# Gate and up products of both feed-forwards by token, their result turned on TensorE, and the input's squares on ScalarE

## Chip, cores and metric

The kernel runs on one core of a Trainium2 chip. The metric is the device time of one execution in microseconds, the median of several runs. Shares and durations come from one profiled execution.

## What is computed

One layer of a streaming encoder on 256 tokens of width 2048, all in float32. The part that the change touches is the two feed-forwards, at the start and at the end:

```python
def rms_norm(x, g):
    y = x * lax.rsqrt(jnp.mean(x * x, axis=-1, keepdims=True) + RMS_EPS)
    return y * g

def swiglu_ffn(h, w_in, w_out):
    gate, up = jnp.split(h @ w_in, 2, axis=-1)      # w_in (2048, 2 * 5632)
    return (jax.nn.silu(gate) * up) @ w_out         # w_out (5632, 2048)

x = x + 0.5 * swiglu_ffn(rms_norm(x, ffn1_norm), ffn1_w_in, ffn1_w_out)
x = x + token_mixing(x)            # convolution and gated MLP, w_mix_in, w_mix_out
x = x + cross_attention(x, mem)    # four heads, w_q, w_k, w_v, w_o
x = x + 0.5 * swiglu_ffn(rms_norm(x, ffn2_norm), ffn2_w_in, ffn2_w_out)
out = rms_norm(x, final_norm)
```

## The kernel before

Every large product runs in float32r. Both operands are split into a high part and a low part that add up to the float32 value, and a product is the sum of three: high by high, high by low, low by high. `weights` (line 97) loads a weight tile of up to 128 x 1024 numbers (512 KB) on SyncE's queue into one of four `raw` buffers. ScalarE casts it to the high part (line 104), and VectorE subtracts for the low part (line 105), both into one of three `hl` buffers. The activations stand in SBUF by feature, `x_hl[:, k]` being 128 features by both parts by 256 tokens; the norm's gain is in them, and its inverse root is multiplied in after the product.

A product comes in three forms. `product` (line 115), which `gemm_t` uses, has 128 weight columns stationary. One matmul moves the 512 columns of both parts of x past the high weights, a second the 256 columns of the high part past the low weights; the result stands by feature, in two halves that are still to be added. `product_joint` (line 120) does the same as three matmuls of 256. `gemm_n` (line 150) has 128 tokens of x stationary and moves 512 weight columns, three matmuls for each k and half of the tokens; its result stands by token. `ffn2_w_out`, `w_mix_v` and `w_v` use it.

`swiglu_in` (line 245) makes a feed-forward's first stage. For each of 44 tiles of 128 hidden features it runs two `gemm_t`, gate and up, of 16 k each (two weight tiles each). The results are joined, multiplied by the inverse root, put through Silu, multiplied and split into `hA` and `hB`, the operands of the second product, all by feature and in operations of 256 columns on ScalarE and VectorE (lines 261 to 269). `first_pair` (line 279) does the first two products of feed-forward 1 while x arrives; GpSimd squares x there (lines 307 and 309), and a product by `ones` (line 208) sums the squares over partitions for the inverse root. Feed-forward 2 takes its sum of squares from `residual` (line 235) of the stage before.

PSUM has six buffers for accumulators (`ps`) and two for small things (`pa`). Small pieces of other work, such as the memory's squares in feed-forward 1 and the transposition of x in blocks of 32 in feed-forward 2 (line 709), are given out by `beside` after weight tiles. The order on each engine is made by a scheduler when the program is built. It follows the program's order, and may put an instruction earlier where an engine would be free.

Of the kernel before, what the change touches and what calls it, by code (L numbers as in the profile page):

```python
# [11 lines left out]
F32 = mybir.dt.float32  # L12
# [23 lines left out]
# columns of the packed per-channel parameters  # L36
# [25 lines left out]
def layer(ctx: ExitStack, tc: tile.TileContext, a: dict):  # L62
# [34 lines left out]
    def weights(src, kk, n, hl=None):  # L97
        """src [P, kk, n] in DRAM: both parts, each [P, kk, n]."""
# [16 lines left out]
    def product(acc, w_hi, w_lo, x_hl, first, last):  # L115
        """acc[:, 0] + acc[:, 1] += w.T @ x, x as [K, 2, n] of both parts."""
# [3 lines left out]
    def product_joint(acc, w_hi, w_lo, x_hl, first, last):  # L120
        """acc[:, 0] += w.T @ x"""
# [5 lines left out]
    def product_part(acc, w, k0, kk, x_hl, per, first, last, joint=False):  # L127
        """The part of a product by feature that k0 .. k0 + kk bring."""
# [6 lines left out]
    def gemm_t(w, x_hl, per=0.0, acc=None, ks=None, joint=False):  # L135
        """w [P, K, 128] in DRAM; x_hl(k) -> [P, 2, 256]: 128 outputs by 256 tokens."""
        return ahead([w], x_hl, per, [acc], ks, joint)[0]

    def ahead(ws, x_hl, per=0.0, accs=None, ks=None, joint=False, end=True):
        """Products of which each part of K is done for all before the next."""  # L140
# [4 lines left out]
        for i, (k0, kk) in enumerate(ks):  # L145
            for w, acc in zip(ws, accs):
                product_part(acc, w, k0, kk, x_hl, per, i == 0 and not started, end and i == len(ks) - 1, joint)
        return accs

    def gemm_n(w, x_hl, per=0.0):  # L150
        """w [P, K, 512] in DRAM: two tiles of 128 tokens by 512 outputs."""
        acc = [ps.tile([P, 2, 256], F32, name="acc").rearrange("p a b -> p (a b)") for _ in range(2)]
        nk = w.shape[1]
        for k0 in range(0, nk, 2):
            kk = min(2, nk - k0)
            hi, lo = weights(w[:, k0:k0 + kk, :], kk, 512)
            for k in range(kk):
                x = x_hl(k0 + k)
                for t in range(2):
# [3 lines left out]
                    nc.tensor.matmul(acc[t], lhsT=x[:, 1, s], rhs=hi[:, k], start=False, stop=k0 + k == nk - 1)  # L163
            beside(per)
        return acc

    def joined(acc, dst):
        """dst = acc[:, 0] + acc[:, 1]"""
# [16 lines left out]
    def inverse_root(dst, src, scale, eps):  # L185
        """dst = (src * scale + eps) ** -0.5, the table's root refined by a Newton step"""
# [18 lines left out]
    def over_partitions(acc):  # L205
        """The sum of acc over partitions, on each partition, in PSUM."""
# [17 lines left out]
    def gained(dst, k, x, g):  # L224
        """dst[:, k] = both parts of x * g"""
# [19 lines left out]
    def swiglu_in(x_hl, root, w_in, hA, hB, first, hold, per):  # L245
        """root() gives the norm's inverse root, after the products of `hold` pairs more than the first."""
        waiting = []
        r = None
        for j in range(KF):
            if j == 0:  # L250
                accs = first()
            else:
                accs = [gemm_t(w_in[j, i], lambda k: x_hl[:, k], per=per if j > 4 else 0.0) for i in range(2)]
            waiting.append((j, accs))
            if j < hold:
                continue
            if r is None:
                r = root()
            for i, (gate, up) in waiting:
                tg = ev.tile([P, T], F32, name="tg")  # L260
                tu = ev.tile([P, T], F32, name="tu")
                joined(gate, tg)
                nc.vector.tensor_tensor(out=tg, in0=tg, in1=r, op=ALU.mult)
                nc.scalar.activation(out=tg, in_=tg, func=AF.Silu)
                joined(up, tu)
                nc.vector.tensor_tensor(out=tu, in0=tu, in1=r, op=ALU.mult)
                nc.vector.tensor_tensor(out=tu, in0=tu, in1=tg, op=ALU.mult)
                dst = hA[:, i] if i < KD else hB[:, i - KD]
                split(dst[:, 0], dst[:, 1], tu)
            waiting = []  # L270
# [8 lines left out]
    def first_pair():  # L279
        """The first two products, as x arrives."""  # L280
        accs = [ps.tile([P, 2, 256], F32, name="acc") for _ in range(2)]
        head = PV["mix_norm"][0]
        for k0 in range(0, KD, 2):
            nc.sync.dma_start(out=xT[:, k0:k0 + 2], in_=a["xT"][:, k0:k0 + 2])
            if k0 == 0:
                nc.sync.dma_start(out=pv[:, :head], in_=a["pv"][:, :head])
            if k0 == 4:
                nc.sync.dma_start(out=pv[:, head:], in_=a["pv"][:, head:])
            raw = wraw.tile([P, 1024], F32, name="raw")
            hl = whl.tile([P, 2, 1024], F32R, name="hl")  # L290
            nc.sync.dma_start(
                out=raw[:, :512].rearrange("p (g k n) -> p g k n", g=2, k=2),
# [557 lines left out]
```

## Time and profile before

| | us |
|---|---|
| median of 3 runs | 2180.48 |
| range of the runs | 2179.02 to 2180.67 |
| span of the profiled execution | 2178.9 |
| TensorE busy | 2156.7 |
| VectorE busy | 1473.8 |
| ScalarE busy | 1056.8 |

The profiled execution's span is 1.6 us less than the median of the runs. In the profile "PE" is TensorE, "PEld" its weight loads, "DVE" VectorE, "ACT" ScalarE, "POOL" GpSimd and "SP" SyncE. A matmul's record covers its way through the array too, so records overlap; the distance between the starts of two matmuls is what one of them takes of the stream. In a weight stream `acc<-x_hl,hl` the first name after the arrow is the moving operand and the second the stationary one.

### The profile page before, as it was taken

The numbers are of one execution on the slowest core, as the hardware profiler recorded it, in microseconds if no ns is written. First come the engines' busy times: TensorE is split into PE (matmuls) and PEld (weight loads), VectorE is DVE, ScalarE is ACT, GpSimd is POOL, SyncE is SP. The second block draws the span as 40 slices with busy tenths as digits, with TensorE's granted clock in tenths as the row PEclk, the third lists the DMA queues.
The fourth block names the chain that finished last, engine by engine and source line by source line (L and its number), as shares of the span: only waits on it lengthen the run. The fifth ranks groups of instructions, "written<-read, shape, count | busy, mean of one in ns | idle before, by whom it ended". The sixth has DMA issues, their size and how long they took to land.

```text
span 2178.9 us, 31893 instructions
## 1 busy us (share of the span) xinstructions
PE 2156.7 (99%) x12396; PEld 1885.7 (87%) x12396; DVE 1473.8 (68%) x2148; ACT 1056.8 (49%) x1492; POOL 41.5 (2%) x54
## 2 busy tenths in 40 slices
PE   7999999999999999999999999999999999999998
PEld 6888888888888899999888888888888888888886
DVE  7866666665555588888897666777776666654444
ACT  5644444444444454544475455554444444444443
POOL 5000000000000000000000000000000000000000
PEclk9999999999999999999999999999999999999999
DMA  6655555555666675545655544555555555565564
GB/s 207 221 190 187 186 186 187 188 184 183 189 189 189 189 255 191 192 170 183 190 184 193 184 161 141 192 184 186 187 189 183 187 189 186 184 193 187 190 191 147
DMA packets 115798, 408.06 MB, mean 187 GB/s; under 512 B 12864, under 2 KB 15040, under 8 KB 115520
## 3 DMA queue, kind: packets, MB, share of 16 engines
q1 hardware_dynamic: 115360, 405.25, 55.5%
q8 instruction: 97, 1.59, 0.3%
q10 hardware_dynamic: 288, 0.79, 0.1%
q14 instruction: 53, 0.43, 0.1%
HBM read 403.89 MB, written 2.10 MB: 186 GB/s over the span
## 4 chain that ended last, share of the span: by engine, by line
PE 97%; DVE 1%; DMA 1%; issue 0%; ACT 0%; SPq 0%; DVEq 0%
PE acc L117 45%; PE acc L118 23%; PE acc L162 5%; PE acc L161 5%; PE acc L163 5%; PE acc L124 4%; PE acc L123 4%; PE acc L125 4%; PE acc L774 1%; PE acc L775 1%; PE acc L776 1%; DMA raw<-in_ffn_w_in 0%; DVE x_hl L227 0%; DVE hl L105 0%; DVE hl L113 0%
## 5 line engine op out<-in xcount | busy, mean ns | idle before, releaser
L105 DVE TENSOR_TENSOR hl<-raw,hl 128x1024 fp32r<-128x1024 f32 (+2 forms) x755 | 914.6, 1212 | 512.6 <-ACT hl L104 499.1
L104 ACT CAST hl<-raw 128x1024 fp32r<-128x1024 f32 (+2 forms) x755 | 783.9, 1039 | 734.1 <-PE acc L118 392.9
L117 PE MATMUL acc<-x_hl,hl 128*128 128x512 f32 x3072 | 1089.9, 400 | 6.1 <-ACT hl L112 6.0
L118 PE MATMUL acc<-x_hl,hl 128*128 128x256 f32 x3072 | 865.2, 282 | 5.8 <-DVE hl L113 5.5
L117 PEld LDWEIGHTS acc<-x_hl,hl 128*128 128x128 f32 x3072 | 579.3, 189 | 148.4 <-ACT hl L112 6.6
L118 PEld LDWEIGHTS acc<-x_hl,hl 128*128 128x128 f32 x3072 | 582.6, 190 | 9.8 <-DVE hl L113 8.6
L117 PE MATMUL acc<-hB,hl 128*128 128x512 f32 x448 | 156.3, 392 | 0.0
L118 PE MATMUL acc<-hB,hl 128*128 128x256 f32 x448 | 125.3, 280 | 0.0
L169 ACT COPY tg<-acc 128x256 f32<-128x256 f32 x104 | 38.8, 373 | 149.1 <-PE acc L118 149.1
L123 PE MATMUL acc<-x_hl,hl 128*128 128x256 f32 x384 | 108.6, 283 | 0.0
L124 PE MATMUL acc<-x_hl,hl 128*128 128x256 f32 x384 | 108.5, 283 | 0.0
L125 PE MATMUL acc<-x_hl,hl 128*128 128x256 f32 x384 | 108.0, 283 | 0.0
L169 ACT COPY tu<-acc 128x256 f32<-128x256 f32 x88 | 32.8, 372 | 142.7 <-PE acc L118 142.7
L117 PEld LDWEIGHTS acc<-hB,hl 128*128 128x128 f32 x448 | 84.1, 188 | 18.9
L117 PE MATMUL acc<-hA,hl 128*128 128x512 f32 x256 | 91.0, 398 | 0.0
L117 PE MATMUL acc<-o_hl,hl 128*128 128x512 f32 x256 | 90.4, 399 | 0.0
L117 PE MATMUL acc<-y_hl,hl 128*128 128x512 f32 x256 | 89.0, 394 | 0.0
L170 DVE TENSOR_TENSOR tu<-tu,acc 128x256 f32<-128x256 f32 x88 | 37.0, 420 | 71.7 <-ACT tu L169 71.7
L118 PEld LDWEIGHTS acc<-hB,hl 128*128 128x128 f32 x448 | 84.3, 188 | 0.0
L170 DVE TENSOR_TENSOR tg<-tg,acc 128x256 f32<-128x256 f32 x104 | 43.8, 421 | 59.6 <-ACT tg L169 59.3
L123 PEld LDWEIGHTS acc<-x_hl,hl 128*128 128x128 f32 x384 | 73.6, 192 | 0.0
L124 PEld LDWEIGHTS acc<-x_hl,hl 128*128 128x128 f32 x384 | 73.6, 192 | 0.0
(226 smaller groups left out, 2824.3 us busy)
## 6 DMA issues: line engine op xcount, KB each, us to landing
raw<-in_ffn_w_in SPq DMA_DIRECT2D x348, 512.0 KB, 3.6
raw<-in_ffn_w_out SPq DMA_DIRECT2D x120, 512.0 KB, 3.5
raw<-in_ffn_w_out SPq DMA_DIRECT2D x64, 448.0 KB, 3.3
raw<-in_w_mix_in SPq DMA_DIRECT2D x48, 512.0 KB, 3.7
raw<-in_w_k SPq DMA_DIRECT2D x32, 512.0 KB, 3.6
raw<-in_w_v SPq DMA_DIRECT2D x32, 512.0 KB, 3.5
raw<-in_w_mix_out SPq DMA_DIRECT2D x32, 512.0 KB, 3.7
raw<-in_w_q SPq DMA_DIRECT2D x32, 512.0 KB, 3.6
```

The lines of the kernel that those rows point to most:

```text
L104: nc.scalar.copy(out=hl[:, 0, :size], in_=raw[:, :size])
L105: newest[0] = nc.vector.tensor_tensor(out=hl[:, 1, :size], in0=raw[:, :size], in1=hl[:, 0, :size].bitcast(F32), op=ALU.subtract)
L117: nc.tensor.matmul(acc, lhsT=w_hi, rhs=x_hl, start=first, stop=False, skip_group_check=True)
L118: nc.tensor.matmul(acc[:, 0], lhsT=w_lo, rhs=x_hl[:, 0], start=False, stop=last, skip_group_check=True)
L123: nc.tensor.matmul(d, lhsT=w_hi, rhs=x_hl[:, 0], start=first, stop=False, skip_group_check=True)
L124: nc.tensor.matmul(d, lhsT=w_hi, rhs=x_hl[:, 1], start=False, stop=False, skip_group_check=True)
L125: nc.tensor.matmul(d, lhsT=w_lo, rhs=x_hl[:, 0], start=False, stop=last, skip_group_check=True)
L161: nc.tensor.matmul(acc[t], lhsT=x[:, 0, s], rhs=hi[:, k], start=k0 + k == 0, stop=False)
L162: nc.tensor.matmul(acc[t], lhsT=x[:, 0, s], rhs=lo[:, k], start=False, stop=False)
L163: nc.tensor.matmul(acc[t], lhsT=x[:, 1, s], rhs=hi[:, k], start=False, stop=k0 + k == nk - 1)
L169: nc.scalar.copy(out=dst, in_=acc[:, 1])
L170: nc.vector.tensor_tensor(out=dst, in0=dst, in1=acc[:, 0], op=ALU.add)
```

## The change

The first stage of both feed-forwards goes by token. 11 groups of 512 hidden features take the place of 44 tiles of 128. A weight tile now holds one k: 512 gate columns and 512 up columns. For each k, `by_two` runs twelve matmuls of 512 moving columns with x stationary, six for each half of the tokens, into four accumulators. `gated` evicts them by token: Silu on ScalarE straight from PSUM with the inverse root as a scale by token, then one multiplication on VectorE. The result `h` has to stand by feature for the second product, so `turn` transposes it on TensorE, four blocks of 128 x 128 into a small PSUM buffer, and splits it into `hA` or `hB`. The two turns of a group are called after k = 3 and k = 5 of the next group, and those of the last group between the parts of the first product that follows.

In `first_group`, which takes the place of `first_pair`, the squares of x come from a copy of x by token (four loads of 512 KB after k = 8, 10, 12 and 14); ScalarE squares them and sums them along the row. For feed-forward 2 the inverse root by token comes from `rms_cols` after group 0. `gf` is loaded later, into memory that the first stage has left. The weights `ffn1_w_in` and `ffn2_w_in` are laid out anew in DRAM for it, 4 KB in one piece for each partition as before.

```diff
+    def by_two(acc, x, hi, lo, first, last):
+        for t in range(2):
+            s = slice(t * P, (t + 1) * P)
+            for g in range(2):
+                c = slice(g * G, (g + 1) * G)
+                nc.tensor.matmul(acc[t][g], lhsT=x[:, 0, s], rhs=hi[:, c], start=first, stop=False)
+                nc.tensor.matmul(acc[t][g], lhsT=x[:, 0, s], rhs=lo[:, c], start=False, stop=False)
+            for g in range(2):
+                c = slice(g * G, (g + 1) * G)
+                nc.tensor.matmul(acc[t][g], lhsT=x[:, 1, s], rhs=hi[:, c], start=False, stop=last)
+
+    def token_accs():
+        return [[ps.tile([P, 2, 256], F32, name="acc").rearrange("p a b -> p (a b)") for _ in range(2)] for _ in range(2)]
 ...
+        def gated(acc, r):
+            h = pool.tile([P, 2, G], F32, name="h", bufs=2)
+            for t in range(2):
+                nc.scalar.activation(out=h[:, t], in_=acc[t][0], func=AF.Silu, scale=r[:, t:t + 1])
+                nc.vector.scalar_tensor_tensor(
+                    out=h[:, t], in0=acc[t][1], scalar=r[:, t:t + 1], in1=h[:, t], op0=ALU.mult, op1=ALU.mult
+                )
+            return h
+
+        def turn(j, h, half):
+            def go():
+                f = 4 * j + 2 * half
+                dst = hA[:, f:f + 2] if f < KD else hB[:, f - KD:f - KD + 2]
+                tp = pa.tile([P, 2, T], F32, name="aux")
+                for k in range(2):
+                    for t in range(2):
+                        c = slice((2 * half + k) * P, (2 * half + k + 1) * P)
+                        nc.tensor.transpose(out=tp[:, k, t * P:(t + 1) * P], in_=h[:, t, c], identity=ident)
+                split(dst[:, :, 0], dst[:, :, 1], tp)
+            return go
 ...
-        for j in range(KF):
-            if j == 0:
-                accs = first()
+        for j in range(NG):
+            if j == 0 and first is not None:
+                acc = first()
             else:
-                accs = [gemm_t(w_in[j, i], lambda k: x_hl[:, k], per=per if j > 4 else 0.0) for i in range(2)]
+                acc = token_accs()
+                for k in range(KD):
+                    hi, lo = weights(w_in[j, :, k:k + 1], 1, 2 * G)
+                    by_two(acc, x_hl[:, k], hi[:, 0], lo[:, 0], k == 0, k == KD - 1)
+                    if k in (3, 5) and turns:
+                        turns.pop(0)()
+                    beside(per)
             if r is None:
                 r = root()
 ...
+            h = gated(acc, r)
+            turns += [turn(j, h, half) for half in range(2)]
+        return turns
 ...
+    def x_squares(c, tot):
+        raw = wraw.tile([P, 1024], F32, name="raw")
+        nc.sync.dma_start(out=raw, in_=a["x"][c // 2 * P:(c // 2 + 1) * P, c % 2 * 1024:(c % 2 + 1) * 1024])
+        nc.scalar.activation(out=raw, in_=raw, func=AF.Square, accum_out=tot[:, c % 2, c // 2:c // 2 + 1])
 ...
+        for k in range(KD):
+            if k % 2 == 0:
+                nc.sync.dma_start(out=xT[:, k:k + 2], in_=a["xT"][:, k:k + 2])
 ...
+            gained(x_hl, k, xT[:, k], col("ffn1_norm", k))
+            hi, lo = weights(a["ffn1_w_in"][0, :, k:k + 1], 1, 2 * G)
+            by_two(acc, x_hl[:, k], hi[:, 0], lo[:, 0], k == 0, k == KD - 1)
 ...
+            if k >= 8 and k % 2 == 0:
+                x_squares(k // 2 - 4, tot)
+        nc.vector.tensor_tensor(out=r_x, in0=tot[:, 0], in1=tot[:, 1], op=ALU.add)
+        inverse_root(r_x, r_x, 1.0 / D, RMS_EPS)
 ...
-    def x_square(k):
-        sq = ss if k == 0 else ev.tile([P, T], F32, name="sq")
-        nc.gpsimd.tensor_tensor(out=sq, in0=xT[:, k], in1=xT[:, k], op=ALU.mult)
-        if k:
-            nc.gpsimd.tensor_tensor(out=ss, in0=ss, in1=sq, op=ALU.add)
 ...
+            turns = swiglu_in(gate, x_hl, lambda: rms_cols(ss, D, "r_x2"), a["ffn2_w_in"], hA, hB, None, 0.4)
+            finish()
+            acc_0 = gemm_n(a["ffn2_w_out"][0], h, between=turns)
```

## Rows read from the trace of the kernel before

**Rows 1.** The page: busy time by engine, and the chain's shares.
```profile
PE 2156.7 (99%) x12396; PEld 1885.7 (87%) x12396; DVE 1473.8 (68%) x2148; ACT 1056.8 (49%) x1492; POOL 41.5 (2%) x54
...
PE 97%; DVE 1%; DMA 1%; issue 0%; ACT 0%; SPq 0%; DVEq 0%
```
**Rows 2.** Timeline, feed-forward 2 first to last; start us, us, engine, instruction, count.
```profile
1427.48 0.40 PE L117 MATMUL acc<-x_hl,hl 128*128 128x512 f32 x1
...
1925.40 0.62 PE L161 MATMUL acc<-hl,hA 128*128 128x512 f32 x2
```
**Rows 3.** Timeline, `w_mix_v` by token: its first matmul and the next stage's.
```profile
856.95 0.40 PE L161 MATMUL acc<-hl,x_hl 128*128 128x512 f32 x1
...
900.50 0.28 PE L123 MATMUL acc<-m_hl,hl 128*128 128x256 f32 x1
```
**Rows 4.** Timeline, `ffn2_w_out` by token: first with `hB`, next output's first.
```profile
1947.18 0.63 PE L161 MATMUL acc<-hl,hB 128*128 128x512 f32 x2
...
1986.38 0.63 PE L161 MATMUL acc<-hl,hA 128*128 128x512 f32 x2
```
**Rows 5.** Timeline, cross-attention: two transposes inside a pair of matmuls.
```profile
1343.60 0.40 PE L117 MATMUL acc<-o_hl,hl 128*128 128x512 f32 x1
1343.84 0.38 PE L629 MATMUL aux<-ident,e 128*128 128x128 f32 x2
1343.97 0.36 PE L118 MATMUL acc<-o_hl,hl 128*128 128x256 f32 x1
1344.17 0.39 PE L117 MATMUL acc<-o_hl,hl 128*128 128x512 f32 x1
```
**Rows 6.** Groups by line and form: count, busy us, mean ns, idle before.
```profile
L629 PE MATMUL aux<-ident,e 128*128 128x128 f32 x16 | 3.2, 271 | 0.0
...
L104 ACT CAST hl<-raw 128x1024 fp32r<-128x1024 f32 x685 | 719.7, 1051 | 634.4 <-PE acc L118 315.5 <-PE acc L163 139.6 <-issue 66.3
L562 ACT ACTIVATE vv<-acc,r_mt 128x512 f32<-128x512 f32 x8 | 5.5, 686 | 1.7 <-PE acc L163 1.7
L105 DVE TENSOR_TENSOR hl<-raw,hl 128x1024 fp32r<-128x1024 f32 x685 | 840.7, 1227 | 439.4 <-ACT hl L104 426.2
L113 DVE TENSOR_TENSOR hl<-raw,hl 128x512 fp32r<-128x512 f32 x8 | 8.7, 1103 | 0.0
L727 DVE SCALAR_TENSOR_TENSOR x<-acc,x 128x512 f32<-128x512 f32 x8 | 5.2, 685 | 7.0 <-PE acc L776 7.0
L105 DVE TENSOR_TENSOR hl<-raw,hl 128x512 fp32r<-128x512 f32 x6 | 4.1, 690 | 7.5 <-ACT hl L104 7.5
```
**Rows 7.** Timeline, feed-forward 1: first matmuls, longest wait, next stage's first.
```profile
5.97 1.22 PE L117 MATMUL acc<-x_hl,hl 128*128 128x512 f32 x2 [5.97 <-ACT hl L112]
...
8.06 0.63 PE L117 MATMUL acc<-x_hl,hl 128*128 128x512 f32 x1
...
14.38 0.55 PE L117 MATMUL acc<-x_hl,hl 128*128 128x512 f32 x1
...
25.71 0.80 PE L118 MATMUL acc<-x_hl,hl 128*128 128x256 f32 x2 [2.70 <-DVE hl L113]
...
517.95 0.40 PE L117 MATMUL acc<-hA,hl 128*128 128x512 f32 x1
```
**Rows 8.** Windows: length, busy us by engine (PE PEld DVE ACT POOL), clock, DMA, GB/s.
```profile
5.00:10.00 5.00, 3.94 (x10) 2.59 (x10) 3.58 (x6) 2.85 (x6) 3.10 (x5) 1.00 0.94 315
10.00:15.00 5.00, 4.71 (x16) 3.71 (x16) 5.00 (x7) 4.33 (x9) 4.92 (x6) 1.00 1.01 348
25.00:40.00 15.00, 14.29 (x66) 12.37 (x67) 9.38 (x10) 5.55 (x8) 9.21 (x9) 0.77 0.65 211
...
1427.48:1925.40 497.92, 497.92 (x2820) 431.74 (x2819) 344.86 (x477) 243.52 (x355) 0.00 (x0) 1.00 0.54 186
```
**Rows 9.** Timeline, cross-attention: last sum of squares, first product by `ones`.
```profile
1223.00 0.42 DVE L203 TENSOR_TENSOR ss<-ss,sq 128x256 f32<-128x256 f32 x1
...
1228.68 0.28 PE L219 MATMUL aux<-ones,ss 128*128 128x1 f32 x2
```

More of the change, by code (lines that the diff above doesn't have):

```diff
@@ L133, in product_part, with gemm_t, ahead @@
         beside(per)
-    def gemm_t(w, x_hl, per=0.0, acc=None, ks=None, joint=False):
-        return ahead([w], x_hl, per, [acc], ks, joint)[0]
-    def ahead(ws, x_hl, per=0.0, accs=None, ks=None, joint=False, end=True):
+    def gemm_t(w, x_hl, per=0.0, acc=None, ks=None, joint=False, between=None):
+        return ahead([w], x_hl, per, [acc], ks, joint, between=between)[0]
+    def ahead(ws, x_hl, per=0.0, accs=None, ks=None, joint=False, end=True, between=None):
         started = accs is not None and accs[0] is not None
@@ L147, in ahead, with gemm_n @@
                 product_part(acc, w, k0, kk, x_hl, per, i == 0 and not started, end and i == len(ks) - 1, joint)
+                if between and i > 0:
+                    between.pop(0)()
         return accs
-    def gemm_n(w, x_hl, per=0.0):
+    def gemm_n(w, x_hl, per=0.0, between=None):
         acc = [ps.tile([P, 2, 256], F32, name="acc").rearrange("p a b -> p (a b)") for _ in range(2)]
@@ L163, in gemm_n @@
                     nc.tensor.matmul(acc[t], lhsT=x[:, 1, s], rhs=hi[:, k], start=False, stop=k0 + k == nk - 1)
+            if between and k0 >= 4:
+                between.pop(0)()
             beside(per)
@@ L242, in residual @@
         square_into(ss, xT[:, f], f == 0)
-    def swiglu_in(x_hl, root, w_in, hA, hB, first, hold, per):
-        waiting = []
+    G = 512
+    NG = F // G
+    def by_two(acc, x, hi, lo, first, last):
[8 more added lines that the diff above has]
+                nc.tensor.matmul(acc[t][g], lhsT=x[:, 1, s], rhs=hi[:, c], start=False, stop=last)
@@ new lines, in token_accs, with swiglu_in @@
+    def token_accs():
+        return [[ps.tile([P, 2, 256], F32, name="acc").rearrange("p a b -> p (a b)") for _ in range(2)] for _ in range(2)]
+    def swiglu_in(pool, x_hl, root, w_in, hA, hB, first, per):
+        turns = []
+        def gated(acc, r):
[17 more added lines that the diff above has]
+            return go
@@ L257, in swiglu_in @@
             if r is None:
                 r = root()
[L259 to L269, printed above, removed]
@@ L288, in first_pair @@
                 nc.sync.dma_start(out=pv[:, head:], in_=a["pv"][:, head:])
[L289 to L292, printed above, removed]
-                in_=a["ffn1_w_in"][0][:, :, k0:k0 + 2, :].rearrange("g p k n -> p g k n"),
-            )
-            for k in range(k0, k0 + 2):
-                gained(x_hl, k, xT[:, k], col("ffn1_norm", k))
-                x_square(k)
@@ L334, in layer @@
         for f in range(KD):
-            acc = gemm_t(a["ffn1_w_out"][f], h_of(hA, hB))
+            if f == 0:
+                acc = gemm_t(a["ffn1_w_out"][f], h_of(hA, hB), between=turns)
+            else:
+                acc = gemm_t(a["ffn1_w_out"][f], h_of(hA, hB))
             residual(acc, f, 0.5, x_hl, "mix_norm", ss)
@@ L712, in turn @@
             return go
+        h = h_of(hA, hB)
         put(0.6, *[turn(i, j) for i in range(4) for j in range(8)])
-        swiglu_in(
-            x_hl, lambda: rms_rows(ss, D, "r_x"), a["ffn2_w_in"], hA, hB,
-            lambda: ahead([a["ffn2_w_in"][0, i] for i in range(2)], lambda k: x_hl[:, k]), 0, 0.3,
-        )
-        finish()
-        h = h_of(hA, hB)
+        with tc.tile_pool(name="gate2", bufs=1) as gate:
+            turns = swiglu_in(gate, x_hl, lambda: rms_cols(ss, D, "r_x2"), a["ffn2_w_in"], hA, hB, None, 0.4)
+            finish()
+            acc_0 = gemm_n(a["ffn2_w_out"][0], h, between=turns)
+        late = stack.enter_context(tc.tile_pool(name="late", bufs=1))
+        gf = late.tile([P, D], F32, name="gf")
+        nc.sync.dma_start(out=gf, in_=a["final_norm"].partition_broadcast(P))
         sums = st.tile([P, 2, 4], F32, name="sums")
@@ L729, in add_up @@
             )
-            sq = pool.tile([P, 512], F32, name="sq2")
+            sq = late.tile([P, 512], F32, name="sq2")
             nc.scalar.activation(out=sq, in_=x2[:, t, s], func=AF.Square, accum_out=sums[:, t, i:i + 1])
@@ L756, in layer @@
         for n in range(3):
-            acc = gemm_n(a["ffn2_w_out"][n], h)
+            acc = gemm_n(a["ffn2_w_out"][n], h) if n else acc_0
             for t in range(2):
```

38 lines of the change are left out of this document (14 added, 24 removed).

## The prediction

> **What bounds the kernel now.** I read the page's busy times and its chain first: TensorE is busy for 99% of the span and 97% of the chain that ended last is TensorE [rows 1]. So no other engine is worth speeding up in itself; a change pays if it shortens the stream of matmuls, or if it takes idle time or a slow clock out of it. Next I looked at the stream in the timeline, stage by stage, at starts and not at durations: the records overlap, and what a matmul costs is the distance to the next start. In feed-forward 2 the 1408 pairs of `product` (512 columns with the high weights, 256 with the low) run from 1427.48 to 1925.40 us [rows 2]: 497.92 / 1408 = 0.3536 us a pair, one small product by `ones` included. Both feed-forwards have this stage, so some 996 us of the span are such pairs. The by-token form, which the change brings there, is already in the trace: the 192 matmuls of 512 columns with `w_mix_v` have `x_hl` stationary and `hl` moving and run from 856.95 to 900.50 [rows 3], 43.55 / 192 = 0.2268 us each.
>
> **Pace of the products.** Columns streamed don't change: 1408 x (512 + 256) = 1,081,344 before, 11 groups x 16 k x 12 matmuls x 512 = 1,081,344 after. What changes is the number of instructions, 2816 before and 2112 after for each feed-forward. From the rows, one weight tile of 512 KB costs 8 x 0.3536 = 2.829 us as pairs and 12 x 0.2268 = 2.722 us by token. For a feed-forward that is 497.9 against 2112 x 0.2268 = 479.0, so -18.9 us, and -37.8 us for both. The row is close: the same operands at the same shapes, read from the same tiles; only the order differs (two PSUM tiles take turns, where `gemm_n` does three matmuls on one). The other end comes from the same form with `hB` stationary: 28 k of `ffn2_w_out`, 168 matmuls from 1947.18 to 1986.38 [rows 4], 0.2333 us each; at that pace a feed-forward takes 492.7 and both gain only 10.4 us. I take the `x_hl` row, since `x_hl` is what is stationary.
>
> **Transposes.** New: 11 groups x 2 halves x 4 = 88 for each feed-forward, 176 in all, on TensorE in the middle of the stream. Two such transposes stand between a pair in cross-attention: from the `product` at 1343.60 to the next at 1344.17 is 0.57 us [rows 5], where a pair alone takes 0.35 [rows 2]; so 0.22 for two, 0.11 each, and 176 x 0.11 = +19.4 us. Four in a row, as here, are not in the trace. Bounds: 0.06, a quarter of the 0.2268 us of 512 columns [rows 3], and 0.27, the mean record of a transpose [rows 6], if nothing of it overlapped; 10.6 to 47.5 us in all. I take 0.11, since it is a distance between starts on a busy engine.
>
> The Trainium skill ("TensorE: Matmul & The Clock Gate", Part 4) speaks against the change here: it puts a 128x128 transpose in a kernel's context at about 275 ns. The records agree (271 ns), the distances don't (110 ns). By that figure the transposes would cost 48 us, more than the pace gives.
>
> **Evictions and splits.** They leave TensorE's stream, and ScalarE and VectorE get lighter: four times eleven operations of 256 columns for a group of four j become two Silu and two VectorE products from PSUM of 512 columns, and two splits of 512. In the stage VectorE is busy 344.86 of 497.92 us [rows 8], so nothing there ends last before or after: nothing gained. What is new is a deadline. A group holds four of the six `acc` buffers. The next one starts on the two free ones and needs those of the first 128 tokens 6 x 0.2268 = 1.36 us later; their last matmul ended 1.36 us before the group's end. So Silu (like L562's, 0.69) and the product (like L727's, 0.69) [rows 6] have 2.7 us for 1.4 us of work. Queued around them are one cast (1.05) and one subtraction (1.23) for each weight tile. I count 0 for 20 boundaries, with +1.5 us altogether for table loads and odd waits.
>
> **Start.** Feed-forward 1 begins its matmuls at 5.97 and ends at 517.95 [rows 7]; against 497.9 of steady pairs its surplus is 20.0 us. The rows say where from: VectorE's subtraction of 512 columns takes 1103 ns as L113 while GpSimd squares x, and 690 ns as L105 later [rows 6]; TensorE waits for it, 2.70 us at the worst [rows 7]; and its 512-column matmuls last 0.63 us, at the lower clock level, up to the first shorter one at 14.38 [rows 7]; after the longest wait the level falls again, and the granted clock of 25 to 40 us is 0.77 on the mean [rows 8]. The change takes GpSimd's squares away (ScalarE squares x by token) and gives each k 2.72 us of TensorE work against 1.23 us of subtraction [rows 6] and one short operation for x on VectorE, so the stream should stop starving. New surplus: first matmul at 5.97 + 0.8 (256 KB more at the 315 to 348 GB/s of [rows 8]) + 0.4 (longer cast) = 7.2; 0.8 until the low part is there; half of some 8.4 us at the lower level, 4.2; the loads of x (2 MB more from k = 8 on: 512 x 12 + 128 x 8 KB in 21.8 us is 330 GB/s, at the top of what the rows show), 0 to 4, taken 1.5; the root, two loads of ScalarE's tables and the memory's squares, now packed behind four consecutive tiles, at the first boundary, 0 to 7, taken 3. Together 16.7, so -3 us (bounds -9 to +4).
>
> **The root of feed-forward 2** now comes after group 0 in the code. If its four tiny products stayed there, the first eviction would wait for product, root, table loads and Newton step, some 5 us from the group's end, against the 1.36 us until the buffers are due: a stall of 3.5 us, and as much again if the clock falls. But in cross-attention the same products (L219) were scheduled at 1228.68, 5 us after the sum was ready at 1223.00 [rows 9] and long before their place in the code. Bounds 0 to +7; I take +1.
>
> **What has no price.** The first result's turns at the end of each stage go between the parts of the next product, k 40 to 43 of which come last; `gf` now loads during `ffn2_w_out`, 60 us before its use; weight loads keep 512 KB in pieces of the same length. Nothing there waits.
>
> Sum: -37.8 + 19.4 + 1.5 - 3 + 1 = -18.9 us. The profiled span is 2178.9, the median run 2180.5, 1.6 us more; 2178.9 - 18.9 + 1.6 gives 2161.6, rounded to 2162.
>
> **Rivals.**
> (a) *Boundary stall, slower.* If ScalarE's queue has the cast of the next tile ahead of Silu, and that cast waits for an `hl` buffer which only the group's last matmul frees, Silu starts 1.05 us after the end and the product behind VectorE's 1.23: 3.7 us from the end, minus 1.36, up to 2.3 us of idle TensorE; at 1.7 on the mean, 20 boundaries cost 34 us: 2162 + 32 = 2194. It decides from 0.95 us a boundary. For it: both queues run in order, and the slack is 1.3 us where the pairs had several. Against: TensorE has no idle time at all in feed-forward 2 now [rows 8], so the order there has always put evictions where they fit. Chance 0.10.
> (b) *Pace of `hB`.* 0.2333 instead of 0.2268: 27.4 us less gain, 2189, slower. For it: the same form runs at two paces, with no cause that I can see. Against: every by-token row whose stationary tile is `x_hl` is at 0.227. Chance 0.09.
> (c) *Transposes at their whole record*, 0.27: +28 us, 2190. The mechanism would be four in a row with no long matmul between to cover their loads. Against: the two in [rows 5] were also neighbours. The skill's figure above is this case. Chance 0.05.
> (d) *Start and roots at their upper bounds*, DMA short from k = 8 on, both first evictions late and the clock down after them: +8 to +12, 2170 to 2174, still faster. Chance 0.12.
> (e) *It doesn't do what it says*: the sum of such parts lands at no change, 2180. Chance 0.02.
>
> **How the numbers follow.** Forecast 0.62 at 2162. Its own bounds: start at its best and transposes a little cheaper, 2150; (d) reaches to 2174. What lies above, (a) to (c), is 0.24; half stalls and paces between the two rows lie in reach, so the upper end goes to 2184, which leaves about 0.2 out. A measurement of this kernel tells some 0.2%, 4 us, from no change. Faster: 0.62 + 0.12 = 0.74. Within 0.2%: (e) and partial (a) and (b), 0.07. Slower: the rest of (a) to (c), 0.19.
>
> **What would show it.** In the profile after: 12 matmuls of a weight tile 2.72 us apart (2.80 is (b)); feed-forward 2's stage some 489 us; four transposes in about 0.45 us, 1.1 is (c); TensorE's idle time in feed-forward 2 near 0, with 1 to 2 us before each group's seventh matmul under (a), ended by VectorE or ScalarE; the first matmul near 7 us, the first group's end near 57, no GpSimd work in it, and the lower clock level once. The prediction is wrong in kind if the stages after feed-forward 1 or 2 change by more than 2 us: I count nothing there.

## The result and the profile after

The changed kernel takes 2159.47 us (2157.44 to 2160.25), beside 2179.75 (2178.31 to 2180.67) for the kernel before on the same chip: a ratio of 0.9904 with an interval of 0.989 to 0.9918. That is 20.3 us less; the forecast was 18.9 less. The profiled execution spans 2158.4 us.

One thing has to stand next to this. The kernel before has two levels of its own: on the chips of the experiments its runs lie either near 2168.5 or near 2179.5 us. The profile that [rows 1 to 9] come from is of the upper level, and so were all four runs beside the result. Against the lower level the change brings some 9 us and not 20. Which stage makes the levels is shown below (`e11`, `e12`).

The page of after, its busy line and the shares of the chain, answering to [rows 1]:

```profile
PE 2137.0 (99%) x11164; PEld 1829.0 (85%) x11164; DVE 1311.4 (61%) x1705; ACT 996.0 (46%) x1232; POOL 13.3 (1%) x23
...
PE 95%; DMA 2%; DVE 1%; issue 1%; ACT 1%; SPq 0%; DVEq 0%; ACTq 0%
```

TensorE is the bound as before, with 1232 matmuls fewer. VectorE has 162 us less to do and ScalarE 61.

The timeline of after: the first matmuls, the first of feed-forward 1's second product, the first that follows feed-forward 2's first stage. They answer to [rows 2, 7].

```profile
7.33 2.07 PE L258 MATMUL acc<-hl,x_hl 128*128 128x512 f32 x4 [7.33 <-ACT hl L104]
9.20 1.05 PE L259 MATMUL acc<-hl,x_hl 128*128 128x512 f32 x2
10.05 0.69 PE L262 MATMUL acc<-hl,x_hl 128*128 128x512 f32 x2
10.58 0.63 PE L259 MATMUL acc<-hl,x_hl 128*128 128x512 f32 x2
11.05 0.62 PE L262 MATMUL acc<-hl,x_hl 128*128 128x512 f32 x2
...
502.24 0.39 PE L117 MATMUL acc<-hA,hl 128*128 128x512 f32 x1
...
1904.64 0.62 PE L163 MATMUL acc<-hl,hA 128*128 128x512 f32 x2
```

Windows of after (length, busy us of PE, PEld, DVE, ACT, POOL, granted clock, DMA share, GB/s), answering to [rows 8]:

```profile
5.00:10.00 5.00, 2.67 (x6) 2.15 (x7) 2.84 (x4) 3.04 (x5) 0.00 (x0) 1.00 1.00 351
...
25.00:40.00 15.00, 15.00 (x68) 12.43 (x67) 4.81 (x4) 8.17 (x11) 0.00 (x0) 1.00 0.72 238
1415.72:1904.64 488.92, 488.92 (x2199) 404.36 (x2197) 266.72 (x258) 211.01 (x223) 0.00 (x0) 1.00 0.64 189
```

The last row is feed-forward 2's first stage: 488.92 us, all of it busy. Before it was 497.92. The clock column reads 1.00 in the first row only because the trace has no record of the clock before 10.19 us (14.70 in the kernel before). The starts above tell the level there: two matmuls take 0.85 us from 9.20 on, and 0.47 from 10.58 on.

Where the 20.4 us between the two spans went, by the starts of the stages on TensorE:

| stage | before | after | difference |
|---|---|---|---|
| until the first matmul | 5.97 | 7.33 | +1.4 |
| feed-forward 1, first product | 511.98 | 494.91 | -17.1 |
| feed-forward 1, second product | 245.97 | 247.97 | +2.0 |
| `w_mix_in` | 93.03 | 95.15 | +2.1 |
| rest of token mixing, cross-attention | 570.53 | 570.36 | -0.2 |
| feed-forward 2, first product | 497.92 | 488.92 | -9.0 |
| feed-forward 2, second product | 253.47 | 253.81 | +0.3 |

Groups of after by line and form (count, busy us, mean ns, idle before): the new operations.

```profile
L288 PE MATMUL aux<-ident,h 128*128 128x128 f32 x176 | 29.7, 272 | 0.0
...
L275 DVE SCALAR_TENSOR_TENSOR h<-acc,r_x,h 128x512 f32<-128x512 f32 x44 | 32.9, 751 | 4.8 <-ACT h L274 4.8
L274 ACT ACTIVATE h<-acc,r_x 128x512 f32<-128x512 f32 x44 | 29.9, 687 | 14.3 <-PE acc L262 14.3
```

The timeline of TensorE around two turns in feed-forward 2:

```profile
1509.64 0.38 PE L288 MATMUL aux<-ident,h 128*128 128x128 f32 x2
1509.78 1.17 PE L258 MATMUL acc<-hl,x_hl 128*128 128x512 f32 x4
1510.79 0.38 PE L288 MATMUL aux<-ident,h 128*128 128x128 f32 x2
1510.92 0.70 PE L259 MATMUL acc<-hl,x_hl 128*128 128x512 f32 x2
1511.47 0.63 PE L262 MATMUL acc<-hl,x_hl 128*128 128x512 f32 x2
1511.93 0.62 PE L259 MATMUL acc<-hl,x_hl 128*128 128x512 f32 x2
1512.39 0.63 PE L262 MATMUL acc<-hl,x_hl 128*128 128x512 f32 x2
1512.86 0.60 PE L288 MATMUL aux<-ident,h 128*128 128x128 f32 x4
1513.21 1.17 PE L258 MATMUL acc<-hl,x_hl 128*128 128x512 f32 x4
```

Between 1509.64 and 1513.21 us lie twelve long matmuls and eight transposes. Twelve times 0.2268 is 2.72, so 0.85 us are left for eight: 0.106 each, though each one's record is 272 ns. One of the two fours was pulled apart into twos (1509.64 and 1510.79) by the scheduler.

The timeline of ScalarE, VectorE and TensorE at one of the boundaries between groups:

```profile
1503.27 0.69 ACT L274 ACTIVATE h<-acc,r_x 128x512 f32<-128x512 f32 x1 [0.53 <-PE acc L262]
1504.17 0.69 ACT L274 ACTIVATE h<-acc,r_x 128x512 f32<-128x512 f32 x1 [0.22 <-PE acc L262]
1504.76 1.04 ACT L104 CAST hl<-raw 128x1024 fp32r<-128x1024 f32 x1
...
1502.77 1.23 DVE L105 TENSOR_TENSOR hl<-raw,hl 128x1024 fp32r<-128x1024 f32 x1 [0.76 <-ACT hl L104]
1503.99 0.75 DVE L275 SCALAR_TENSOR_TENSOR h<-acc,r_x,h 128x512 f32<-128x512 f32 x1
1504.89 0.75 DVE L275 SCALAR_TENSOR_TENSOR h<-acc,r_x,h 128x512 f32<-128x512 f32 x1 [0.15 <-ACT h L274]
...
1502.84 0.62 PE L262 MATMUL acc<-hl,x_hl 128*128 128x512 f32 x2
...
1504.20 0.62 PE L258 MATMUL acc<-hl,x_hl 128*128 128x512 f32 x2
```

The product of the first half starts at 1503.99 and is done at 1504.74. It starts 0.03 us after its Silu's end, as the second half's product does (1504.86 and 1504.89). The subtraction ahead of it on VectorE ends at 1503.99 too, so its wait there can't be told from the wait for Silu and cost nothing that shows. The next group begins at 1504.20, and its seventh matmul, the first that needs this buffer, comes six of 0.2268 later, at 1505.56. So 0.8 us of slack was left where the prediction counted 1.3. Most of the difference went before Silu: the last matmul of its accumulator starts at 1502.84 and its record ends at 1503.23, 0.97 us before the next group and not 1.36. The scheduler had put two matmuls of the second half ahead of it.

### The profile page after: what moved, and what is told of

Read it like the earlier page. It is cut to its first block, busy times and chain, and to the rows that moved or that the text cites. A ratio compares the mean times of both kernels' runs of the same rounds, so it can differ in the third digit from the quotient of the medians.

```text
span 2158.4 us, 28547 instructions
## 1 busy us (share of the span) xinstructions
PE 2137.0 (99%) x11164; PEld 1829.0 (85%) x11164; DVE 1311.4 (61%) x1705; ACT 996.0 (46%) x1232; POOL 13.3 (1%) x23
## 4 chain that ended last, share of the span: by engine, by line
PE 95%; DMA 2%; DVE 1%; issue 1%; ACT 1%; SPq 0%; DVEq 0%; ACTq 0%
PE acc L117 16%; PE acc L258 14%; PE acc L262 14%; PE acc L259 14%; PE acc L118 8%; PE acc L165 5%; PE acc L163 5%; PE acc L164 5%; PE acc L125 3%; PE acc L124 3%; PE acc L123 3%; PE acc L811 1%; PE acc L813 1%; PE acc L812 1%; PE aux L288 1%; DMA raw<-in_x 1%
## 5 line engine op out<-in xcount | busy, mean ns | idle before, releaser
L259 PE MATMUL acc<-hl,x_hl 128*128 128x512 f32 x1408 | 446.2, 391 | 0.5 <-DVE hl L105 0.5
L262 PE MATMUL acc<-hl,x_hl 128*128 128x512 f32 x1408 | 440.7, 390 | 0.0
L258 PE MATMUL acc<-hl,x_hl 128*128 128x512 f32 x1408 | 395.3, 393 | 9.7 <-ACT hl L104 8.0
L258 PEld LDWEIGHTS acc<-hl,x_hl 128*128 128x128 f32 x1408 | 261.6, 188 | 62.5 <-ACT hl L104 8.5
L262 PEld LDWEIGHTS acc<-hl,x_hl 128*128 128x128 f32 x1408 | 264.5, 188 | 55.4
L259 PEld LDWEIGHTS acc<-hl,x_hl 128*128 128x128 f32 x1408 | 262.8, 188 | 55.1 <-DVE hl L105 1.4
L123 PE MATMUL acc<-x_hl,hl 128*128 128x256 f32 x384 | 108.7, 283 | 0.5 <-ACT hl L104 0.5
L125 PE MATMUL acc<-x_hl,hl 128*128 128x256 f32 x384 | 108.2, 283 | 0.9 <-DVE hl L105 0.7
L124 PE MATMUL acc<-x_hl,hl 128*128 128x256 f32 x384 | 108.5, 283 | 0.0
L117 PEld LDWEIGHTS acc<-hB,hl 128*128 128x128 f32 x448 | 84.1, 188 | 20.4
L117 PE MATMUL acc<-x_hl,hl 128*128 128x512 f32 x256 | 90.6, 396 | 0.0
L125 PEld LDWEIGHTS acc<-x_hl,hl 128*128 128x128 f32 x384 | 73.4, 192 | 1.3 <-DVE hl L105 1.3
L123 PEld LDWEIGHTS acc<-x_hl,hl 128*128 128x128 f32 x384 | 73.7, 192 | 0.8 <-ACT hl L104 0.7
L124 PEld LDWEIGHTS acc<-x_hl,hl 128*128 128x128 f32 x384 | 73.7, 192 | 0.0
```

Source lines behind the costliest of these rows:

```text
L117: nc.tensor.matmul(acc, lhsT=w_hi, rhs=x_hl, start=first, stop=False, skip_group_check=True)
L123: nc.tensor.matmul(d, lhsT=w_hi, rhs=x_hl[:, 0], start=first, stop=False, skip_group_check=True)
L124: nc.tensor.matmul(d, lhsT=w_hi, rhs=x_hl[:, 1], start=False, stop=False, skip_group_check=True)
L125: nc.tensor.matmul(d, lhsT=w_lo, rhs=x_hl[:, 0], start=False, stop=last, skip_group_check=True)
L258: nc.tensor.matmul(acc[t][g], lhsT=x[:, 0, s], rhs=hi[:, c], start=first, stop=False)
L259: nc.tensor.matmul(acc[t][g], lhsT=x[:, 0, s], rhs=lo[:, c], start=False, stop=False)
```

## Experiments

The theory is the prediction's sum: by-token products at 0.2268 us, transposes at 0.11, nothing lost at the boundaries, a start that no longer starves. The first four runs test those terms and the rivals (b), (c) and (a); the next four test what the traces then left open (the first boundary, and why the same form has two paces); the last four test the readings themselves. `e4_squares` and the kernels named with "before" are changes of the kernel before, all others of the changed kernel. Differences are read from stages, since a stage doesn't carry the two levels of another one.

### e1_no_turn: the transposes alone

```diff
-                tp = pa.tile([P, 2, T], F32, name="aux")
-                for k in range(2):
-                    for t in range(2):
...
-                        nc.tensor.transpose(out=tp[:, k, t * P:(t + 1) * P], in_=h[:, t, c], identity=ident)
-                split(dst[:, :, 0], dst[:, :, 1], tp)
+                split(dst[:, :, 0], dst[:, :, 1], h[:, :, half * T:(half + 1) * T])
```

> The changed kernel without its 176 transposes: the splits read h as it stands by token, so the result is not the layer's. The first theory prices a transpose at the distance between starts, 0.11 to 0.12 us: the time falls by 19 to 21 us to about 2139, feed-forward 2's first stage from 488.9 to about 479.3 us. The rival, a transpose at its whole record of 0.27 us, expects 45 us less, 2114. If transposes were hidden behind waits, nothing changes.

2139.56 us (2138.14 to 2140.32), 19.9 less than the changed kernel: 19.9 / 176 = 0.113 us a transpose. Feed-forward 2's first stage in its windows:

```profile
1404.28:1883.51 479.23, 479.23 (x2118) 397.13 (x2117) 266.87 (x258) 211.54 (x223) 0.00 (x0) 1.00 0.65 193
```

479.23 / 2112 is 0.2269 us a matmul, the pace of [rows 3]. Against 488.92 with the 80 transposes that lie in this stage (the last eight lie in the next) one costs 9.69 / 80 = 0.121 us. Rival (c), 0.27 each, would have made 47 us of it; it falls.

### e2_evict_late: the other half of the tokens first

```diff
-            for t in range(2):
+            for t in (1, 0):
                 nc.scalar.activation(out=h[:, t], in_=acc[t][0], func=AF.Silu, scale=r[:, t:t + 1])
```

> The changed kernel with the second half of the tokens evicted before the first. The theory that the buffers of the first half are due 1.36 us after a group's end expects them some 2.3 to 2.9 us after it, so 0.9 to 1.5 us of idle TensorE at each of 20 boundaries, 18 to 30 us more, about 2178 to 2190. If evictions have several us to spare, as with pairs, the time stays within 2 us of 2159.

2160.46 us (2158.0 to 2161.74), no change. It tells nothing about the deadline: at the same boundary Silu starts at 1503.94, 0.94 us before the next group's first matmul at 1504.88, and in the changed kernel 0.93 us before it (1503.27 and 1504.20). So the edit did not make this eviction later. The scheduler probably issues the Silu whose accumulator is complete first. Rival (a) is settled by the slack and by the missing idle time of the changed kernel itself; how much later an eviction may come was not measured.

### e3_ff2_only: feed-forward 1 as before

Feed-forward 1 keeps `swiglu_in`, `first_pair` and GpSimd's squares of the kernel before. A pad of 32 bytes lets both `hB` begin where they do in the changed kernel.

> Only feed-forward 2 by token; feed-forward 1 and its squares as before. If the two feed-forwards gain as their stages show, 9 us from feed-forward 2 and 15 from the other with its start and what follows, this runs at about 2171 (-9). If the gain came from the start and the squares alone, it stays at 2180.

2172.28 us (2171.68 to 2174.32). Feed-forward 2's stage is 488.94, as in the changed kernel, and feed-forward 1's is 512.34, as in the kernel before. So neither half of the change alters the other's first stage: 9.0 us come from the one, against the upper level of the kernel before, and the rest, 12.8 us between 2172.28 and 2159.47, from the other. Against the lower level, near 2168.5, `e3` is 3.8 us slower: there feed-forward 2's stage took 488.54 already (`e11`), so that by token it gains nothing.

### e4_squares: the kernel before, only x's squares taken from GpSimd

```diff
     def x_square(k):
-        sq = ss if k == 0 else ev.tile([P, T], F32, name="sq")
-        nc.gpsimd.tensor_tensor(out=sq, in0=xT[:, k], in1=xT[:, k], op=ALU.mult)
-        if k:
-            nc.gpsimd.tensor_tensor(out=ss, in0=ss, in1=sq, op=ALU.add)
+        square_into(ss, xT[:, k], k == 0)
```

> The kernel before with the squares of x on ScalarE and their sum on VectorE instead of GpSimd, all else as before. The first theory has GpSimd slow VectorE's subtraction (1103 against 690 ns) and TensorE waiting for it; then feed-forward 1's first stage loses part of its 14 us of surplus, 4 to 8 us, and the time is 2172 to 2176. If the loads or the small weight tiles of the start set its pace, the time stays within 2 us of 2180.

2169.1 us on the median, in two groups, 2162.8 to 2165.0 and 2173.2 to 2175.1. The kernel before had 2167.0 to 2170.1 and 2177.6 to 2182.1 beside it, so each group fell by some 5 us. Its group of VectorE's subtraction of 512 columns, and its windows of 25 to 40 us and of feed-forward 2's first stage:

```profile
L113 DVE TENSOR_TENSOR hl<-raw,hl 128x512 fp32r<-128x512 f32 x8 | 5.3, 688 | 1.0 <-ACT hl L112 0.8
...
25.00:40.00 15.00, 15.00 (x86) 13.05 (x85) 12.44 (x21) 9.79 (x12) 0.00 (x0) 1.00 0.68 231
...
1420.52:1909.07 488.55, 488.55 (x2821) 431.43 (x2819) 344.99 (x477) 243.58 (x355) 0.00 (x0) 1.00 0.57 190
```

The same L113 took 1103 ns in [rows 6], beside GpSimd's squares. Without them it takes 688, TensorE is busy for all of 25 to 40 us at the upper clock level (0.77 on the mean in [rows 8]), and feed-forward 1's first product falls from 511.98 to 505.69 us. So GpSimd's squares cost 6.3 us of this stage without any by-token form; 5.7 are left at its end, since the first matmul comes 0.6 later, at 6.59. The Trainium skill ("SBUF — State Buffer", "Who interferes with whom") says that a VectorE instruction with two SBUF inputs contends with a GpSimd instruction that reads SBUF; both of L113's inputs are in SBUF, and the two means, 1103 and 688 ns, agree.

The last row was not expected. Feed-forward 2 is untouched in this kernel and takes 488.55 us instead of 497.92: 0.3470 us a pair, not 0.3536. This opened the question that `e11` and `e12` answer.

### e5_shift_hB and e7_shift_x: where a stationary operand begins

In the built program `x_hl` and `hA` begin at bytes 20032 and 52800 of each partition, multiples of 64; `hB` begins at 144928 in the changed kernel and 144864 in the kernel before, 32 past one. These addresses stand in no trace; the sizes of the tiles in the kernels give the same distances. They could be the cause of the two paces of rival (b). In `e5` a pad moves everything behind the small tiles on by 32, both `hB` among it. In `e7` two pads move `x_hl` and `hA` on by 32, and the weight tiles and `hB` by 64.

```diff
+    fit = ctx.enter_context(tc.tile_pool(name="fit", bufs=1))
+    nc.vector.memset(fit.tile([P, 8], F32, name="fit"), 0.0)
     pa = ctx.enter_context(tc.tile_pool(name="pa", bufs=2, space=bass.MemoryType.PSUM))
```

```diff
+    low = ctx.enter_context(tc.tile_pool(name="low", bufs=1))
+    nc.vector.memset(low.tile([P, 8], F32, name="low"), 0.0)
     big = ctx.enter_context(tc.tile_pool(name="big", bufs=2))
+    mid_fit = ctx.enter_context(tc.tile_pool(name="mid_fit", bufs=1))
+    nc.vector.memset(mid_fit.tile([P, 8], F32, name="mid_fit"), 0.0)
```

> The changed kernel with everything behind the small tiles, hB among it, 32 bytes further in SBUF, so that hB begins on a multiple of 64 bytes as hA and x_hl do. If the slower pace of matmuls with hB stationary (0.2333 against 0.2268 us) comes from where hB begins, the 672 matmuls of the last product gain 4.4 us, about 2155. If it comes from hB lying far up in SBUF or from the work beside it, the time stays at 2159.

> The changed kernel with x_hl, hA, y_hl and o_hl 32 bytes further in SBUF, off the multiple of 64 bytes, and the weight tiles and hB 64 bytes further, which leaves them where they were in this respect. If the stationary operand's place sets the pace, the by-token products with x_hl go from 0.2268 to about 0.2333 us, 27 us more in the two feed-forwards and 6 in w_mix_v, w_v and hA's part, about 2192. If not, the time stays at 2159.

`e5`: 2157.06 us (2156.37 to 2158.04). Its window of the first 168 matmuls with `hB` stationary, the stretch of [rows 4]:

```profile
1929.24:1967.32 38.08, 38.08 (x169) 31.53 (x168) 17.36 (x15) 14.77 (x14) 0.00 (x0) 1.00 0.67 194
```

38.08 / 168 = 0.2267 us, where [rows 4] gave 39.20 / 168 = 0.2333. The last stage falls from 253.81 to 249.33. Feed-forward 1's second product, where `hA` and `hB` are the moving operands, became 1.6 us longer, and nearly all of that lies in the pairs with `hA`, which had not moved: 16 of them take 5.65 us instead of 5.56, 28 with `hB` 9.89 instead of 9.88.

`e7`: 2190.24 us (2189.11 to 2191.31), slower than the kernel before by 1.007 (1.0042 to 1.0098). Its window of feed-forward 2's first stage:

```profile
1431.62:1933.53 501.91, 501.91 (x2198) 403.79 (x2197) 266.84 (x258) 210.17 (x223) 0.00 (x0) 1.00 0.62 185
```

13.0 us more than in the changed kernel with the same instructions; without the 9.69 us of transposes it is 0.2331 us a matmul, where 488.92 gives 0.2269. Rival (b) was a real mechanism. Its price, 2189, is near what this kernel measures, though 25 of the 31 us lie in the two first stages that it was counted for, and the rest elsewhere. What decided against it in the changed kernel is where `x_hl` happens to begin, by itself or against the weights: `e7` moved those too, from 64 past a multiple of 128 bytes to a multiple of 128.

### e6_memory_later: the memory's squares out of the first group

The timeline of ScalarE at the first boundary of the changed kernel, then TensorE's there:

```profile
48.04 1.03 ACT L104 CAST hl<-raw 128x1024 fp32r<-128x1024 f32 x1
51.45 0.42 ACT L203 ACTIVATE sm<-raw 128x256 f32<-128x256 f32 x1 [2.38 <-DMA raw<-in_memT]
51.78 0.71 ACT L206 ACTIVATE sq<-raw 128x256 f32<-128x256 f32 x2
52.39 1.98 ACT L104 CAST hl<-raw 128x1024 fp32r<-128x1024 f32 x2
55.11 0.87 ACT L206 ACTIVATE sq<-raw 128x256 f32<-128x256 f32 x2 [0.74 <-DVE sm L207]
56.00 1.28 ACT L274 ACT_TABLE_LOAD   x1
57.29 1.27 ACT L274 ACTIVATE h<-acc,r_x 128x512 f32<-128x512 f32 x2
...
53.47 0.73 PE L258 MATMUL acc<-hl,x_hl 128*128 128x512 f32 x2 [0.71 <-ACT hl L104]
54.73 0.73 PE L259 MATMUL acc<-hl,x_hl 128*128 128x512 f32 x2 [0.53 <-DVE hl L105]
...
58.03 0.50 PE L258 MATMUL acc<-hl,x_hl 128*128 128x512 f32 x1 [1.64 <-ACT h L274]
```

ScalarE stands for 2.38 us on the memory's load, with the next weight tile's cast queued behind it; the table load for Silu and Silu itself come after that. TensorE loses 0.71 + 0.53 + 1.64 = 2.9 us. The edit gives the memory's squares out from the fourth group on:

```diff
-                    beside(per)
+                    if j > 2 or w_in is not a["ffn1_w_in"]:
+                        beside(per)
```

> The changed kernel with the memory's squares from the fourth group on instead of behind the first four weight tiles of the second. TensorE was idle for 2.9 us in three pieces between 52 and 58 us, with ScalarE's queue behind the memory's squares and their load. The theory that those squares hold up the cast and the first Silu expects 2 to 3 us less, about 2157. If the first Silu waits for its table or the root in any case, 0 to 1 us.

2156.07 us (2155.08 to 2157.43). ScalarE's timeline at the same place:

```profile
49.51 1.05 ACT L104 CAST hl<-raw 128x1024 fp32r<-128x1024 f32 x1 [0.53 <-DMA raw<-in_ffn_w_in]
51.56 1.05 ACT L104 CAST hl<-raw 128x1024 fp32r<-128x1024 f32 x1 [1.00 <-DMA raw<-in_ffn_w_in]
52.63 1.28 ACT L274 ACT_TABLE_LOAD   x1
53.93 1.27 ACT L274 ACTIVATE h<-acc,r_x 128x512 f32<-128x512 f32 x2
```

The table load starts at 52.63 instead of 56.00, TensorE's waits there are gone but for 0.13 us, and the stage falls from 494.91 to 491.40 us.

### e8_both and e9_shift_hB2: put together

`e8` has the edits of `e5` and `e6`. `e9` has that of `e6` and a pad ahead of feed-forward 2's `hB` alone.

```diff
+        fit = stack.enter_context(tc.tile_pool(name="fit", bufs=1))
+        nc.vector.memset(fit.tile([P, 8], F32, name="fit"), 0.0)
         pool = stack.enter_context(tc.tile_pool(name="ffn2", bufs=1))
```

> The changed kernel with both edits, hB on a multiple of 64 bytes and the memory's squares later. If both theories hold, 6 to 7 us less than the changed kernel, about 2153; if one holds, 2155 to 2157.

> The changed kernel with the memory's squares kept out of the first group (as in e6) and a pad of 32 bytes ahead of feed-forward 2's hB alone, so that it starts on a multiple of 64 bytes while feed-forward 1's stays where it was. By the theory that a stationary operand off such a multiple costs 6.67 ns for each 512-column matmul: 28 k x 6 matmuls x 4 outputs = 672 matmuls x 6.67 ns = 4.5 us less than e6 (2156.1), so 2151.6, with the last stage at 249.3 us (253.8 without) and feed-forward 1's output stage at 248.0 as in e6. It should be some 1.6 us below e8, whose pad also moved feed-forward 1's hB and cost 1.6 us there. Against it: if the gain of e5 came from the shift of feed-forward 1's buffers, the last stage stays at 253.8 and the time at 2156.

`e8`: 2154.12 us (2153.01 to 2155.3), 5.4 less than the changed kernel where 6 to 7 were expected; its pad costs 1.6 in feed-forward 1's second product, as in `e5`. `e9`: 2151.05 us (2149.55 to 2152.64), the fastest kernel that computes the layer, with a ratio of 0.9896 (0.9869 to 0.9923) to the kernel before on its chip, whose runs there were of both levels. Its window of the stretch of [rows 4]:

```profile
1922.50:1960.58 38.08, 38.08 (x170) 31.53 (x168) 17.36 (x15) 14.77 (x14) 0.00 (x0) 1.00 0.67 194
```

The last stage is 249.33 us and feed-forward 1's second product 247.97, both as expected: the gain of `e5` comes with feed-forward 2's `hB`, its loss with what its pad moves in feed-forward 1.

### e10_before_hB2: the same pad in the kernel before

The pad stands ahead of the pool `ffn2` there.

> The kernel before with the same pad ahead of feed-forward 2's hB. The last stage is by token in the kernel before too, so the same theory gives 672 x 6.67 ns = 4.5 us off it: 253.5 to 249.0 us, the spacing with hB stationary 233.3 to 226.7 ns, nothing else. Whole time 4.5 us under whichever of its two levels the kernel before shows beside it (2168 to 2170 or 2178 to 2181).

2166.43 us (2164.32 to 2167.53 in eight runs, 2173.74 and 2175.52 in two), so it has the two levels as well, each a few us lower. The window of the stretch of [rows 4]:

```profile
1935.88:1974.33 38.45, 38.45 (x169) 31.55 (x168) 17.40 (x15) 14.66 (x14) 0.00 (x0) 1.00 0.66 191
```

38.45 / 168 = 0.2289, between the two paces known so far, and the last stage is 250.27 us, 3.2 less and not 4.5. Here `hB` begins at 144896, a multiple of 128; in `e5` and `e9` at 144960, 64 past one, as `x_hl` and `hA` are in every kernel but `e7`. So "a multiple of 64" is not the whole rule. The three paces seen are 226.7 ns at 64 past a multiple of 128, 228.9 at a multiple of 128, and 233.3 at 32 or 96 past one. The moving weights begin at 64 past one in each kernel but `e7`, where they begin at a multiple of 128 and `x_hl`, `hA` and `hB` at 96 past one, all three at 233. Whether the position itself counts or its distance from the moving operand's is open: every pace here fits both.

### e11_before_again and e12_before_again: the kernel before, profiled twice more

> The kernel before, unchanged, for a second profile. Its runs fall in two groups, near 2168.5 and near 2179.5 us. If the pace of the pairs is what separates them, the spacing of feed-forward 2's pairs is 0.3536 us and its stage 498 us in a run near 2179.5, and 0.3470 us and 488.6 us in a run near 2168.5. If the groups come from elsewhere (start, loads), the stage is 498 us in both.

> The same as e11, a third profile of the kernel before: stage of feed-forward 2's pairs 498 us in a run near 2179.5 us, 488.6 us in one near 2168.5, by the theory that the pace of the pairs is what has two levels; 498 us in either case by the theory that the difference lies elsewhere.

2169.84 and 2169.69 us, the lower level in both. The window of feed-forward 2's pairs in `e11`:

```profile
1426.00:1914.54 488.54, 488.54 (x2821) 430.70 (x2819) 344.81 (x477) 243.67 (x355) 0.00 (x0) 1.00 0.57 190
```

The stage of [rows 2] with the same program: 488.54 us instead of 497.92, no idle time in either, the clock at 1.00 in both. `w_o`, which is made of pairs too, takes 100.67 instead of 101.99. These two make 10.7 us of the 10.8 between the spans, 2178.88 and 2168.04. So the level is the pace of the pairs: 0.3470 or 0.3536 us. The upper level rests on the one profile of [rows 2]. Feed-forward 1's pairs ran at 0.3533 in `e11` and `e12`, as in that profile. In the traces of both levels the pace changes back and forth in cross-attention, where TensorE waits near 1332 and 1348 us; soon after the second wait the one trace settles at the slower pace, the other at the faster, and both hold it to the end of feed-forward 2. What picks the one or the other is open. The kernels with feed-forward 2 by token have the same two paces in what is left of such pairs there: `w_o` takes 101.8 to 102.1 us in the changed kernel, `e5`, `e7` and `e8`, and 100.5 to 100.6 in `e1`, `e2`, `e3`, `e6` and `e9`.

## Why the prediction was right, step by step

**Pace of the products: the by-token side right, the pairs' side half the story.** 479.0 us was worked out for a feed-forward without transposes; `e1` measures 479.23. But the 497.92 that it was set against is one of two levels of one program. Against 488.54 the pace is worth 9.3 us in feed-forward 2 and not 18.9, and there the transposes eat all of it: 488.92 after, 488.54 before. The one stretch of [rows 2] was taken as the form's price, and a second execution would have shown another. In feed-forward 1 the term of 18.9 stands: its pairs ran at 0.3533 in every profile that has them. It was luck that the kernel before ran at its upper level in all four runs beside the result; about half of its runs on the other chips did not, and against those a gain of 18.9 would have been twice the measured one.

**Transposes: right.** 19.4 us expected, 19.9 measured by `e1` (20.1 in the four stages that hold transposes); 0.113 each over the whole and 0.121 in the stage, beside 0.11 from [rows 5]. The distance between starts was the price, and the record of 272 ns was not. The 275 ns of the Trainium skill ("TensorE: Matmul & The Clock Gate", Part 4), a figure for bf16, agree with that record, not with what a transpose takes of this stream.

**Evictions and boundaries: right, with less room than counted.** No idle time in feed-forward 2, so the 1.5 us for odd waits were not needed. At the boundary shown the slack was 0.8 us instead of 1.3, mostly because Silu could start only 0.93 us before the next group. Neither thing that rival (a) feared came there: the next tile's cast stands behind both Silu in ScalarE's queue, at 1504.76, and the subtraction on VectorE is over by the time the product's Silu lets it start. The prediction counts eleven operations of 256 columns for each j; lines 261 to 269 have ten, and nothing hung on it.

**Start: direction right, its size too small.** The surplus over the steady stage was 20.0 and is 7.33 + 494.91 - 488.9 = 13.3, so -6.7 and not -3. The first matmul came at 7.33 (7.2 expected), and the first boundary lost 2.9 us (3 taken). What was mis-sized are the two middle terms, 4.2 for the lower clock level and 1.5 for loads: in after, the first six 512-column matmuls take 2.72 us, from 7.33 to 10.05, twice the 1.36 of the upper level, and from 10.58 on they go at that level. So the lower one cost some 1.4 us, where half of 8.4 had been taken over from before. Between the first matmul and the first boundary, near 52 us (57 was named), TensorE has no idle time, and the 25 to 40 us window is at the upper level throughout: the loads cost nothing. The boundary's 3 us had the right size for a wrong reason: not the root, but the memory's load at the head of ScalarE's queue (`e6`). And `e4` shows that most of the start's gain needs none of the by-token form.

**Root of feed-forward 2: +1 taken, 0 found.** The square root ran at 1429.64 us, 14 us into group 0 and long before that group's end, as with L219 in [rows 9], and the first eviction waited for nothing.

**No price elsewhere: wrong by some 3 us.** The prediction's own sign of being wrong in kind was 2 us for a stage after either feed-forward, and `w_mix_in` passes it. Feed-forward 1's second product grew by 2.0; `e1`, at 247.14, puts 0.8 of that on the eight transposes that spill into it, counted in the sum already. The rest is the pairs' pace, 5.56 us instead of 5.65 for 16 with `hA` and 9.88 instead of 9.73 for 28 with `hB`. It comes with where the tiles begin and not with the by-token form: `e3`, with feed-forward 1 as before and `hB` where the changed kernel has it, takes 247.14 too. `w_mix_in` grew by 2.1: TensorE, which had no idle time there, waits three times for 1.4 us in all, with ScalarE waiting for its loads (4.6 us to landing for the median load, 3.7 before). It varies: 93.03 to 93.60 in three profiles of the kernel before, 93.81 to 95.23 in the eight kernels with both feed-forwards by token, and 94.15 in `e3`. That cause was not tested. This loss takes back most of the start's extra gain, so the total came closer than the steps did, which is luck too.

## What to carry to other kernels

Price an operation in a busy stream by the distance between starts, and take that distance from more than one execution: the pace of one program's pairs differed by 1.9% between runs, half of what was gained on it. Before making a matmul form the main one, look where its stationary operand begins in SBUF and time it there; pads of 32 bytes took 4.5 us off one stage (`e9`) and added 31 us to the whole (`e7`). And when ScalarE evicts, keep work that waits for a load out of its queue near the eviction.

## What the runs showed that was not expected

- Where the stationary operand begins in SBUF, by itself or against the moving one, changes the pace of a 512-column float32r matmul: 226.7, 228.9 or 233.3 ns (`e5`, `e7`, `e9`, `e10`), with the same instructions and no idle time.
- One and the same program runs its pairs of 512 and 256 columns at 0.3470 or 0.3536 us, whole stages long, at the same granted clock (`e11`, `e12` and [rows 2]). It is worth 10.7 us of 2180. In the kernels with both feed-forwards by token `w_o` still shows it, worth some 1.3 us, and their runs spread by 4 us at most.
- A subtraction on VectorE of 512 columns takes 1103 ns beside GpSimd's squares and 688 without (`e4`).
